# RWKV-7 recurrence: alpha and key times a stored by the inverse stage and loaded by the recurrence, y normalised on ScalarE

## The chip, the cores and the metric

The kernel runs on one core of one Trainium2 chip. The metric is the device time of one execution in microseconds (us), and of several executions the median. A core has TensorE (PE, with a separate stream of weight loads, PEld), VectorE (DVE), ScalarE (ACT), GpSimd (POOL) and SyncE (SP). In this kernel SP issues the DMA transfers between DRAM and the on-chip memory.

## The reference, cut to what matters

The reference is one inference step of a trunk with two layers. Layer 0 is a gated DeltaNet, layer 1 is RWKV-7 time mixing with D = 1024 and 16 heads of 64. The input is one prompt of 16 + 1024 tokens and 8 sample sequences of 8 tokens. The change touches layer 1 alone, and there the recurrence and the group norm behind it:

```python
kk = l2norm((k * k_k).reshape(B, T, H, N))
k = k * (1.0 + (a - 1.0) * k_a)
decay = jnp.exp(-jnp.exp(w))
b_h = kk * a_h

def step(S, inp):
    r_t, k_t, v_t, d_t, kk_t, b_t = inp
    S = (S * d_t[:, :, None, :]
         + jnp.einsum('bhvk,bhk->bhv', S, -kk_t)[..., None] * b_t[:, :, None, :]
         + v_t[..., None] * k_t[:, :, None, :])
    return S, jnp.einsum('bhvk,bhk->bhv', S, r_t)

S, y = lax.scan(step, S0, ...)
mean = jnp.mean(y, -1, keepdims=True)
var = jnp.mean(jnp.square(y - mean), -1, keepdims=True)
y = (y - mean) * lax.rsqrt(var + GN_EPS) * lnx_w + lnx_b
y = y + jnp.sum(r_h * k_h * r_k, -1, keepdims=True) * v_h
y = y.reshape(B, T, D) * jax.nn.silu(z)
return y @ w_o, S, xn[:, -1]
```

Every token's state update depends on the one before. The kernel does it in chunks of 64 tokens. Within a chunk, with D the running product of the decays, it uses four scaled rows: alpha = kk times D of the token before, r times D, k divided by D, and kk times a divided by D. Products of these give the triangular matrices of a chunk, and one of them has to be inverted.

## The kernel before, in words

All tokens stand in 1104 columns, cut into three segments of 384, 384 and 336. The 16 RWKV heads are taken in 8 pairs, one head in each half of the 128 partitions. A head pair in one segment is an item; there are 24 of them, numbered 8 times the segment plus the pair, and each has six chunks of 64.

Layer 0 takes the first 1380 us or so of the span. Layer 1 then has two stages.

In the first, up to about 1850 us, `layer1` makes the projections of the keys with decay and rate, then 24 calls of `project` for r, v and the gate's part z. They are numbered 0 to 23; each multiplies one 1024x128 block of weights with all columns and stores its result to DRAM (rd, vd, zd). `load_w` (L198) brings such a block in two halves of 256 KB (tile wraw, 2 buffers); ACT casts the high part (whi, L86), POOL makes the low part (wlo, L90), and PE uses both (3 buffers each). A half block takes part in 36 matmuls. Behind projections 0, 3, 6, 9 and 12 `rwkv_inverse` treats a batch of five items (the last one four). Per item it loads decay sums, a and k, makes kk (ACT), D and 1/D (`Dp`, `iD`, ACT), alpha (tile sal, DVE L1280, with small copies on POOL), kk times a (POOL L1305) and that over D (tile skk, DVE L1306), and multiplies them on PE: 12 small matmuls fL, with three more, frss, for the norms of kk. The result goes through DRAM (store L1319) into blocks of 32x32 of all items of the batch. DVE inverts these row by row (L448 and L450, a chain of 31 steps for all blocks at once), the results go through invA and DRAM to the tiles r_t and r_u (loads L472 and L471), and PE merges them to inverses of 64x64 (mU, mY), which are stored to ttd (L1332). In this stage a scheduler with a model of the times sets the order of every engine. SP has one queue, and carries out its issues in that order: the weights, the loads of the items, the stores.

The second stage, from about 1850 us to the end, is `wave`: the recurrence. It runs over steps tau from -3 to 54; item n has its chunk ci at step tau = 2n + ci, so three items are under way at a time, and a new one begins every second step. The order on PE is written out by hand, that on the other engines is the scheduler's. For each item:

- `rwkv_front` runs ahead, at tau 2n-4. It loads decay sums, k, a, r and v, makes kk, D and 1/D again, and from them the tile AR (alpha, POOL L1280 to L1283, and r times D, DVE L1358) and the tile BK (k over D, DVE L1365, and kk times a over D, POOL L1362 and L1366). AR has 5 buffers, BK has 2.
- At tau 2n-2 and 2n-1 the parts follow: the products BK by AR, masked into G (DVE L1395, L1397), the bonus (pr L1371, rbv L1380), values into UV, the inverse from ttd, and BK transposed into BT (L1407).
- `step_solve` to `step_state` do a chunk: PE products into rA, ACT makes X and UV and the scaled old state pre (all L62) and copies y (L1490; L1488 on DVE for the first chunk), DVE updates the state S (L1484, L1486).
- `rwkv_finish`, at the last chunk: mean and variance (DVE L1503 and L1504), the inverse root (`rsqrt`, tile grs, L103 to L106), and y minus mean times grs, chunk by chunk on POOL (L1509). Then PE transposes y (fyT), and DVE applies weight, bonus and gate (L1516, L1517).

`fill` puts matmuls of the gate and output projections (zz, zo, do) between these on PE, so that PE need not wait for the recurrence. The sums of the output projections go through DRAM (zst, L1591 to L1607), and the final norm is in `finish` (f2k L1638, dfin).

Of the kernel before, what the change touches and what calls it, by code (L numbers as in the profile page):

```python
# [10 lines left out]
AF = mybir.ActivationFunctionType  # L11
ALU = mybir.AluOpType
# [23 lines left out]
class Builder:  # L36
# [1211 lines left out]
    def rwkv_open(self):  # L1248
        self.rk2 = self.t(self.cp, [128, 144], "rk2")
        self.csd, self.ad, self.rd, self.vd, self.zd, self.kd = (self.dram([8, 128, 1152], n) for n in  # L1250
                                                                 ("csd", "ad", "rd", "vd", "zd", "kd"))
        self.ttd = self.dram([24, 128, 384], "ttd")

    def rwkv_load(self, n, pool, tag, names):
        nc, t = self.nc, self.t
# [9 lines left out]
    def rwkv_keys(self, p, ld, pool, tag):  # L1265

        nc, t = self.nc, self.t
        kk = t(pool, [128, 384], tag + "kk", 2 if tag == "s" else 1)
        self.act(kk, ld["k"], AF.Identity, scale=self.pcol["rwkv_k_k"][:, p:p + 1])
        Dp, iD = t(pool, [128, 385], tag + "Dp", 1), t(pool, [128, 384], tag + "iD", 1)  # L1270
        nc.gpsimd.memset(Dp[:, 0:1], 1.0)
        self.act(Dp[:, 1:385], ld["cs"], AF.Exp, scale=-self.DEC)
        self.act(iD, ld["cs"], AF.Exp, scale=self.DEC)
        return kk, Dp, iD

    def alpha(self, al, kk, Dp, s, eng):

# [10 lines left out]
    def rwkv_inverse(self, b, pool):  # L1288

        items = range(5 * b, min(5 * b + 5, 24))  # L1290
        nth = 6 * len(items)
        nc, t = self.nc, self.t
        ltd, ssd = self.dram([nth, 128, 64], f"rltd{b}"), self.dram([nth, 128], f"rssd{b}")
        for q, n in enumerate(items):
            s, p = divmod(n, 8)
            names = ("cs", "a", "k")
            ld = self.ahead or self.rwkv_load(n, pool, "s", names)
            kk, Dp, iD = self.rwkv_keys(p, ld, pool, "s")

            self.ahead = self.rwkv_load(n + 1, pool, "s", names) if n < 23 else None  # L1300
            sq = t(pool, [128, 384], "sgl", 2)
            self.act(sq, kk, AF.Square)
            al = t(pool, [128, 6, 64], "sal", 1)
            self.alpha(al, kk, Dp, s, nc.vector)
            nc.gpsimd.tensor_tensor(kk, kk, ld["a"], op=ALU.mult)  # L1305
            nc.vector.tensor_tensor(kk, kk, iD, op=ALU.mult)  # L1306
            gp = self.ps("f", 2, "L")
            ssp = self.ps("f", 2, "rss")
            for c in range(6):
                for h in (0, 1):  # L1310
                    a = 64 * h
# [13 lines left out]
        rk2 = self.rk2[:, 30 * b:30 * b + nth]  # L1325
        blk = self.block_scale(ssd, rk2, pool)
        TT = [t(pool, [128, 6, 64], "sTT", 3) for _ in items]
        T1n, L21 = t(pool, [128, 30, 32], "T1n", 1), t(pool, [128, 30, 32], "L21", 1)
        self.inverse_blocks(f"r{b}", ltd, blk, pool, TT, T1n[:, 0:nth], L21[:, 0:nth], nth)
        for q, n in enumerate(items):  # L1330
            self.inverse_merge(L21, TT[q], T1n, rk2[:, 6 * q:6 * q + 6], pool, 6 * q, 6)
            nc.sync.dma_start(self.ttd[n], TT[q].rearrange("p c k -> p (c k)"))  # L1332


    def rwkv_front(self, p, s):

        nc, t, ap, fp, col = self.nc, self.t, self.ap, self.fp, self.pcol
        P = Ctx()
        P.p, P.s, P.n = p, s, 8 * s + p
        NB = self.NB  # L1340
# [6 lines left out]
                q = slice(64 * h, 64 * h + 64)  # L1347
                nc.sync.dma_start(P.TT[q, h].rearrange("p c k -> p (c k)"), self.ttd[P.n][q])
        ld = self.rwkv_load(P.n, fp, "f", ("cs", "k", "a", "r", "v"))
        kk, Dp, iD = self.rwkv_keys(p, ld, fp, "f")  # L1350
        DC = P.DC = t(fp, [128, 14], "DC", NB + 2)
        nc.gpsimd.tensor_copy(DC[:, 0:6].unsqueeze(2), Dp[:, 1:385].rearrange("p (c k) -> p c k", k=64)[:, :, 63:64])
        if s == 0:
            nc.gpsimd.tensor_copy(DC[:, 6:14].unsqueeze(2), Dp[:, 1:65].rearrange("p (c k) -> p c k", k=8)[:, :, 7:8])
        AR = P.AR = t(fp, [128, 6, 2, 64], "AR", NB + 1)
        c6 = lambda x: x.rearrange("p (c k) -> p c k", k=64)
        self.alpha(AR[:, :, 0, :], kk, Dp, s, nc.gpsimd)
        nc.vector.tensor_tensor(AR[:, :, 1, :], c6(ld["r"]), c6(Dp[:, 1:385]), op=ALU.mult)  # L1358
        k2 = t(fp, [128, 384], "k2", 1)
        self.act(k2, ld["a"], AF.Identity, scale=pc("rwkv_k_a"), bias=self.omka[:, p:p + 1])  # L1360
        nc.vector.tensor_tensor(k2, k2, ld["k"], op=ALU.mult)
        nc.gpsimd.tensor_tensor(kk, kk, ld["a"], op=ALU.mult)  # L1362

        BK = t(fp, [128, 6, 2, 64], "BK", 2)
        nc.vector.tensor_tensor(BK[:, :, 0, :], c6(k2), c6(iD), op=ALU.mult)  # L1365
        nc.gpsimd.tensor_tensor(BK[:, :, 1, :], c6(kk), c6(iD), op=ALU.mult)  # L1366
        flat = lambda x: x.rearrange("p x k -> p (x k)")
        yield P

# [14 lines left out]
        def scores(c):  # L1384

            gp = [self.ps("f", 2, "G") for h in (0, 1)]
            for u in range(3):
                for h in (0, 1):
                    q = slice(64 * h, 64 * h + 64)
                    self.mm(gp[h][:, 128 * u:128 * u + 128], flat(BK[q, c + u]), flat(AR[q, c + u]))  # L1390
            for h in (0, 1):
                g3 = gp[h][:, 0:384].rearrange("p (q k) -> p q k", k=128)
                f = 0
                if s == 0 and c == 0:
                    nc.vector.tensor_tensor(G[:, 0, h, :], g3[:, 0, :], self.gms, op=ALU.mult)  # L1395
                    f = 1
                nc.vector.tensor_tensor(G[:, c + f:c + 3, h, :], g3[:, f:3], self.gm.unsqueeze(1).broadcast_to([128, 3 - f, 128]),  # L1397
                                        op=ALU.mult)
# [26 lines left out]
    def step_solve(self, P, ci):  # L1425

        nc, t, ap = self.nc, self.t, self.ap
        c = 6 * P.s + ci
        if ci == 0:
            P.y = t(ap, [128, 6, 64], "y", 4)  # L1430
        AR, S = P.AR, self.S[P.p]
        pA = P.pA = self.ps("r", 3, "A")
        X = P.X = t(ap, [128, 64], "X", 4)
        hs = [slice(0, 64), slice(64, 128)]
        if c > 1:
            for h in (0, 1):
                self.mmx(pA[hs[h], 0:64], AR[hs[h], ci, 0], S[hs[h]], True)
            for h in (0, 1):
                self.mmx(pA[hs[h], 256:320], AR[hs[h], ci, 1], S[hs[h]])

    def step_scores(self, P, ci):
        nc, t, ap = self.nc, self.t, self.ap
# [49 lines left out]
    def rwkv_finish(self, p, s, P):  # L1492

        nc, t, ap, col = self.nc, self.t, self.ap, self.pcol
        c0, n = SEGS[s]
# [4 lines left out]
        mv = t(ap, [128, 6, 2], "mv", 2)  # L1500
        y6 = y
# [3 lines left out]
        va, rs = t(ap, [128, 6], "va", 2), t(ap, [128, 6], "grs", 2)  # L1505
        nc.vector.tensor_scalar(va, mv[:, :, 1], GN_EPS, None, op0=ALU.add)
        self.rsqrt(rs, va, ap, "gn")
        for q in range(6):
            nc.gpsimd.tensor_scalar(y6[:, q], y6[:, q], mv[:, q, 0:1], rs[:, q:q + 1], op0=ALU.subtract, op1=ALU.mult)  # L1509
        yield  # L1510
        yp = self.ps("f", 2, "yT")
        for q in range(6):
# [16 lines left out]
    def rwkv_sample_read(self, P):  # L1529

        nc, t, ap = self.nc, self.t, self.ap
        p, AR = P.p, P.AR
# [12 lines left out]
        rp = self.ps("d", 2, "rsr")  # L1545
        for b in range(8):
            for h in (0, 1):
                a = 64 * h
                self.mm(rp[a:a + 64, 16 * b:16 * b + 16], P.Sb[a:a + 64, b, :], AR[a:a + 64, 0, :, 8 * b:8 * b + 8])
# [368 lines left out]
```

## Time and profile before

| What | Value |
|---|---|
| Runs | 2364.39, 2366.5 and 2373.59 us, median 2366.5 |
| Profiled execution | 2368.36 us, of which the span of the trace is 2366.6 |
| Mean granted TensorE clock | 0.969 |
| PE busy | 2187.2 us, 92% of the span |
| DVE, ACT, POOL busy | 68%, 54%, 46% |
| Bytes moved by the hardware DMA queue | 286.53 MB |

A group of instructions is told by line, engine, operation, the tile written and the tiles read, with its count, busy time, mean duration of one in ns and the idle time of its engine just before it. A wait row says which instruction waited, and for which engine, tile and line. A timeline row gives start, duration, engine, line, operation and tiles; in square brackets stands the wait just before it. The granted clock is the share of full speed that the throttle let TensorE have.

### The profile page before, as it was taken

Reading aid. Unit: us, or ns where it says so; the run is one execution under the profiler, and the core shown is the slowest. Engines: PE = TensorE matmul, PEld = TensorE weight load, DVE = VectorE, ACT = ScalarE, POOL = GpSimd, SP = SyncE. Lnnn points to the kernel's source line nnn. Section 1 sums busy time; section 2 is a strip of 40 time slices with the busy share of each in tenths; the row PEclk is TensorE's granted clock in tenths of the full one; section 3 lists DMA queues with packets and bytes.
Section 4 is the critical chain, followed back from the end, with each engine's and each line's share of the span. In section 5 each row is a group of like instructions: output and inputs, shape, how many; then the busy total and the mean of one; then the engine's idle time right before and its main releaser. Section 6 shows DMA issues by size and latency. Waiting matters only on the chain. (4 is left out here: it accounts for less than half of the span.)

```text
span 2366.6 us, 55058 instructions
## 1 busy us (share of the span) xinstructions
PE 2187.2 (92%) x19833; PEld 1991.7 (84%) x19833; DVE 1605.3 (68%) x4201; ACT 1283.9 (54%) x3665; POOL 1095.3 (46%) x1542
## 2 busy tenths in 40 slices
PE   6989999999999999999999999998899998999896
PEld 5878988888898989887989999897788877778785
DVE  6868668695857686783335833479786566778754
ACT  5455546464655555556333655646444455667663
POOL 3435334443434343444131532545344656777764
PEclk9999999999999999999999999999999989999998
DMA  3324333323233333336153154566754544565544
GB/s 113 106 67 112 83 85 83 108 68 103 87 90 94 88 110 89 85 94 192 50 151 94 44 165 163 169 162 176 203 140 132 176 112 139 159 186 177 176 145 128
DMA packets 471019, 290.06 MB, mean 123 GB/s; under 512 B 188601, under 2 KB 456122, under 8 KB 470746
## 3 DMA queue, kind: packets, MB, share of 16 engines
q1 hardware_dynamic: 470746, 286.53, 42.9%
q8 instruction: 157, 2.57, 0.5%
q14 instruction: 116, 0.95, 0.1%
HBM read 200.53 MB, written 85.89 MB: 121 GB/s over the span
## 5 line engine op out<-in xcount | busy, mean ns | idle before, releaser
L90 POOL TENSOR_TENSOR wlo<-wraw,whi 128x512 fp32r<-128x512 f32 (+2 forms) x252 | 328.0, 1304 | 348.0 <-ACT whi L86 334.1
L76 PE MATMUL d<-xc,whi 128*128 128x384 f32 (+2 forms) x910 | 258.1, 340 | 12.0 <-ACT whi L86 6.7
L86 ACT CAST whi<-wraw 128x512 fp32r<-128x512 f32 (+2 forms) x252 | 151.7, 603 | 139.5 <-PE dq L76 50.6
L415 DVE SCALAR_TENSOR_TENSOR cvy<-raw,cw,cvy 128x408 f32<-128x408 f32 (+2 forms) x288 | 179.5, 637 | 17.2 <-ACT cvy L62 15.4
L76 PEld LDWEIGHTS d<-xc,whi 128*128 128x128 f32 (+1 forms) x910 | 167.7, 191 | 16.7 <-ACT whi L86 7.3
L448 DVE TENSOR_TENSOR invtmp<-invA,invT 72x31 f32<-72x31 f32 (+31 forms) x403 | 166.0, 412 | 14.0 <-DMA invA<-ltd 4.4
L450 DVE TENSOR_TENSOR invT<-invT,invtmp 72x31 f32<-72x31 f32 (+31 forms) x403 | 166.4, 413 | 6.5
L76 PE MATMUL dz<-xc,whi 128*128 128x384 f32 (+1 forms) x480 | 149.9, 343 | 0.0
L76 PE MATMUL dv<-xc,whi 128*128 128x384 f32 (+1 forms) x480 | 146.8, 335 | 0.0
L76 PE MATMUL d<-xc,wlo 128*128 128x384 f32 (+2 forms) x428 | 142.8, 343 | 1.0 <-POOL wlo L90 0.9
L76 PE MATMUL d<-xa,whi 128*128 128x384 f32 (+3 forms) x450 | 139.2, 344 | 4.2 <-DVE xa L90 1.8
L864 POOL TENSOR_SCALAR Sb<-Sb,eglb 128x128 f32<-128x128 f32 x128 | 81.8, 656 | 85.4 <-DMA Sb<-in_state_gdn 29.3
L1509 POOL TENSOR_SCALAR y<-y,mv,grs 128x64 f32<-128x64 f32 x144 | 84.1, 601 | 37.4 <-DVE grs L106 35.8
L76 PE MATMUL dz<-xa,whi 128*128 128x384 f32 (+1 forms) x288 | 101.3, 352 | 0.0
L76 PE MATMUL dv<-xa,whi 128*128 128x384 f32 (+1 forms) x288 | 100.1, 347 | 0.1
L76 PEld LDWEIGHTS dz<-xc,whi 128*128 128x128 f32 x480 | 89.8, 193 | 0.8
L76 PEld LDWEIGHTS d<-xa,whi 128*128 128x128 f32 (+1 forms) x450 | 83.2, 190 | 8.2 <-DVE xa L90 2.4
L76 PEld LDWEIGHTS dv<-xc,whi 128*128 128x128 f32 x480 | 88.6, 188 | 0.5 <-issue 0.4
L76 PE MATMUL d<-xa,wlo 128*128 128x384 f32 (+3 forms) x252 | 86.4, 343 | 0.8 <-POOL wlo L90 0.8
L62 ACT ACTIVATE o<-rA,gcol 128x128 f32<-128x128 f32 x128 | 46.7, 372 | 73.0 <-DVE S L775 72.6
L76 PE MATMUL d<-xh,wlo 128*128 128x384 f32 (+1 forms) x256 | 83.5, 341 | 2.0 <-POOL wlo L90 1.9
L76 PEld LDWEIGHTS d<-xc,wlo 128*128 128x128 f32 (+1 forms) x428 | 80.8, 190 | 4.1 <-issue 1.8
(508 smaller groups left out, 7221.8 us busy)
## 6 DMA issues: line engine op xcount, KB each, us to landing
wraw<-in_gdn_w_in SPq DMA_DIRECT2D x96, 256.0 KB
wraw<-in_rwkv_w_rkvz SPq DMA_DIRECT2D x80, 256.0 KB
Sb<-in_state_gdn SPq DMA_DIRECT2D x64, 256.0 KB
wraw<-in_rwkv_w_o SPq DMA_DIRECT2D x40, 256.0 KB
E<-drow SPq DMA_DIRECT2D x24, 384.0 KB
attn<-drow SPq DMA_DIRECT2D x24, 384.0 KB
wraw<-in_gdn_w_out SPq DMA_DIRECT2D x36, 256.0 KB
out_s_gdn<-Sb SPq DMA_DIRECT2D x32, 256.0 KB
```

The costliest lines, as they stand in the source:

```text
L62: return self.nc.scalar.activation(out, in_, func, bias=bias, scale=scale, **kw)
L76: self.nc.tensor.matmul(out, lhsT, rhs, start=start, stop=stop)
L86: nc.scalar.copy(hi, x)
L90: e.tensor_tensor(lo, x, hi.bitcast(F32), op=ALU.subtract)
L415: nc.vector.scalar_tensor_tensor(y[:, 0:wd], raw[:, k:k + wd], cw[k], y[:, 0:wd], op0=ALU.mult, op1=ALU.add)
L448: nc.vector.tensor_tensor(tmp, A[:, j, j + 1:32].unsqueeze(2).broadcast_to([nb, n, m]), Tv[:, j, 0:m].unsqueeze(1).broadcast_to([nb, n, m] ...
L450: nc.vector.tensor_tensor(Tv[:, j + 1:32, 0:m], Tv[:, j + 1:32, 0:m], tmp, op=ALU.subtract)
L864: nc.gpsimd.tensor_scalar(Sb[:, u], Sb[:, u], self.eglb[:, hv, 4 * g + u:4 * g + u + 1], None, op0=ALU.mult)
L1509: nc.gpsimd.tensor_scalar(y6[:, q], y6[:, q], mv[:, q, 0:1], rs[:, q:q + 1], op0=ALU.subtract, op1=ALU.mult)
```

## The change

The inverse stage stores what it makes anyway: alpha (sal) to a new DRAM tensor ald, and kk times a over D (skk) to bkd, 192 KB each, for all 24 items; 48 stores on SP. `rwkv_front` no longer makes kk, alpha, kk times a and BK's second half, but loads alpha into AR and the other into BK, 48 loads on SP, the latter in runs of 256 bytes. It still makes D and 1/D, r times D and k over D. AR is laid out with alpha and r times D as two planes of six chunks (before, the two stood side by side in each chunk). The tile of kk has two buffers in the one place where it remains, as before. In `rwkv_finish` DVE makes nm = -mean times grs, one instruction per item on 128x6 elements, and the six normalisations per item, 144 in all, are activations on ScalarE with scale grs and bias nm.

By engine, in instructions of the built programs: DVE 4131 to 4155, ACT 3424 to 3544, POOL 1547 to 1299, SP 1922 to 2018; PE has 14353 in both.

```diff
-        self.ttd = self.dram([24, 128, 384], "ttd")
+        self.ttd, self.ald, self.bkd = (self.dram([24, 128, 384], n) for n in ("ttd", "ald", "bkd"))
...
     def rwkv_keys(self, p, ld, pool, tag):
-        kk = t(pool, [128, 384], tag + "kk", 2 if tag == "s" else 1)
+        kk = t(pool, [128, 384], tag + "kk", 2)
         self.act(kk, ld["k"], AF.Identity, scale=self.pcol["rwkv_k_k"][:, p:p + 1])
+        return kk, *self.rwkv_decays(ld, pool, tag)
+
+    def rwkv_decays(self, ld, pool, tag):
         Dp, iD = t(pool, [128, 385], tag + "Dp", 1), t(pool, [128, 384], tag + "iD", 1)
         nc.gpsimd.memset(Dp[:, 0:1], 1.0)
         self.act(Dp[:, 1:385], ld["cs"], AF.Exp, scale=-self.DEC)
         self.act(iD, ld["cs"], AF.Exp, scale=self.DEC)
-        return kk, Dp, iD
+        return Dp, iD
...
             self.alpha(al, kk, Dp, s, nc.vector)
             nc.gpsimd.tensor_tensor(kk, kk, ld["a"], op=ALU.mult)
             nc.vector.tensor_tensor(kk, kk, iD, op=ALU.mult)
+            nc.sync.dma_start(self.ald[n], al.rearrange("p c k -> p (c k)"))
+            nc.sync.dma_start(self.bkd[n], kk)
...
-        kk, Dp, iD = self.rwkv_keys(p, ld, fp, "f")
+        Dp, iD = self.rwkv_decays(ld, fp, "f")
...
-        AR = P.AR = t(fp, [128, 6, 2, 64], "AR", NB + 1)
+        AR = P.AR = t(fp, [128, 2, 6, 64], "AR", NB + 1)
+        BK = t(fp, [128, 6, 2, 64], "BK", 2)
+        nc.sync.dma_start(AR[:, 0].rearrange("p c k -> p (c k)"), self.ald[P.n])
+        nc.sync.dma_start(BK[:, :, 1, :], self.bkd[P.n].rearrange("p (c k) -> p c k", k=64))
-        self.alpha(AR[:, :, 0, :], kk, Dp, s, nc.gpsimd)
-        nc.vector.tensor_tensor(AR[:, :, 1, :], c6(ld["r"]), c6(Dp[:, 1:385]), op=ALU.mult)
+        nc.vector.tensor_tensor(AR[:, 1], c6(ld["r"]), c6(Dp[:, 1:385]), op=ALU.mult)
...
-        nc.gpsimd.tensor_tensor(kk, kk, ld["a"], op=ALU.mult)
-        BK = t(fp, [128, 6, 2, 64], "BK", 2)
         nc.vector.tensor_tensor(BK[:, :, 0, :], c6(k2), c6(iD), op=ALU.mult)
-        nc.gpsimd.tensor_tensor(BK[:, :, 1, :], c6(kk), c6(iD), op=ALU.mult)
...
+        nm = t(ap, [128, 6], "gnm", 2)
+        nc.vector.scalar_tensor_tensor(nm, mv[:, :, 0], -1.0, rs, op0=ALU.mult, op1=ALU.mult)
         for q in range(6):
-            nc.gpsimd.tensor_scalar(y6[:, q], y6[:, q], mv[:, q, 0:1], rs[:, q:q + 1], op0=ALU.subtract, op1=ALU.mult)
+            self.act(y6[:, q], y6[:, q], AF.Identity, scale=rs[:, q:q + 1], bias=nm[:, q:q + 1])
```

The reads of AR in `scores`, `step_old` and the sample read follow the new layout. Every file line behind the first edit moves by a few.

More of the change, by code (lines that the diff above doesn't have):

```diff
@@ L1267, in rwkv_keys @@
         nc, t = self.nc, self.t
-        kk = t(pool, [128, 384], tag + "kk", 2 if tag == "s" else 1)
+        kk = t(pool, [128, 384], tag + "kk", 2)
         self.act(kk, ld["k"], AF.Identity, scale=self.pcol["rwkv_k_k"][:, p:p + 1])
+        return kk, *self.rwkv_decays(ld, pool, tag)
+    def rwkv_decays(self, ld, pool, tag):
+        nc, t = self.nc, self.t
         Dp, iD = t(pool, [128, 385], tag + "Dp", 1), t(pool, [128, 384], tag + "iD", 1)
@@ L1389, in scores @@
                     q = slice(64 * h, 64 * h + 64)
-                    self.mm(gp[h][:, 128 * u:128 * u + 128], flat(BK[q, c + u]), flat(AR[q, c + u]))
+                    self.mm(gp[h][:, 128 * u:128 * u + 128], flat(BK[q, c + u]), AR[q, :, c + u])
             for h in (0, 1):
@@ L1436, in step_solve @@
             for h in (0, 1):
-                self.mmx(pA[hs[h], 0:64], AR[hs[h], ci, 0], S[hs[h]], True)
+                self.mmx(pA[hs[h], 0:64], AR[hs[h], 0, ci], S[hs[h]], True)
             for h in (0, 1):
-                self.mmx(pA[hs[h], 256:320], AR[hs[h], ci, 1], S[hs[h]])
+                self.mmx(pA[hs[h], 256:320], AR[hs[h], 1, ci], S[hs[h]])
     def step_scores(self, P, ci):
@@ L1548, in rwkv_sample_read @@
                 a = 64 * h
-                self.mm(rp[a:a + 64, 16 * b:16 * b + 16], P.Sb[a:a + 64, b, :], AR[a:a + 64, 0, :, 8 * b:8 * b + 8])
+                self.mm(rp[a:a + 64, 16 * b:16 * b + 16], P.Sb[a:a + 64, b, :], AR[a:a + 64, :, 0, 8 * b:8 * b + 8])
         q = t(ap, [128, 2, 8, 8], "rkst", 1)
```

## The prediction

> **What bounds the kernel now.** I read the busy shares first, then busy time by stretches of 100 us, then what TensorE (PE) waited for in layer 1, then the timeline at the two places that the change touches.
>
> ```profile
> PE 2187.2 (92%) x19833; PEld 1991.7 (84%) x19833; DVE 1605.3 (68%) x4201; ACT 1283.9 (54%) x3665; POOL 1095.3 (46%) x1542
> ```
>
> ```profile
> 1600.00:1700.00 100.00, 90.18 (x1045) 80.42 (x1044) 90.31 (x205) 59.59 (x135) 44.70 (x66) 0.95 0.67 179
> 1700.00:1800.00 100.00, 86.86 (x975) 77.89 (x976) 84.26 (x189) 50.57 (x107) 45.63 (x59) 0.95 0.58 148
> 2100.00:2200.00 100.00, 90.34 (x1315) 78.59 (x1315) 80.42 (x218) 66.67 (x214) 76.33 (x98) 0.97 0.61 183
> ```
>
> PE is the bound, at 92% of the span. Columns of the stretches: length, busy PE, PEld, DVE, ACT, POOL, granted clock, DMA share, GB/s. In both stages of the change (inverses about 1500 to 1760, recurrence about 1850 to 2366) PE has 10 to 13 us idle in 100. DVE is second in the inverse stage; in the recurrence DVE and POOL lie close together. Work taken off POOL therefore buys time only where PE waits for it or for what it holds up. What PE waits for, inverse stage first (total, times, longest):
>
> ```profile
> PE d L76 <- ACT whi L86: 6.7, 2, 6.1
> ```
>
> ```profile
> PE fBT L73 <- DVE G L1397: 11.8, 13, 1.2
> PE zz L76 <- DVE zst L1033: 5.3, 2, 2.7
> PE rA L80 <- ACT y L1490: 4.8, 15, 1.0
> PE zo L76 <- DVE zst L1605: 4.5, 3, 2.8
> PE dfin L73 <- DVE f2k L1638: 4.1, 1, 4.1
> PE rA L80 <- DVE y L1488: 2.1, 1, 2.1
> PE do L76 <- DVE f2k L1638: 2.0, 1, 2.0
> ```
>
> The first is a late projection weight; the rest is the recurrence, nearly all behind DVE, none behind POOL.
>
> **The inverse stage: 48 stores in front of the weights.** SP issues loads, stores and weight loads in one fixed order. The change adds two stores of 192 KB per head pair and segment (ald, bkd), and a store waits until DVE has made alpha and kk·a·iD, holding all behind it on SP. The scheduler also moves the weight loads back. Places on SP in the two built programs, half projections:
>
> ```
> weight load    before  after        weight load    before  after
> 12, 1st half   1144    1177         13, 2nd half   1226    1316
> 12, 2nd half   1158    1255         14, 1st half   1236    1318
> 13, 1st half   1224    1292         14, 2nd half   1253    1347
> ```
>
> In the new order, place 1254, just ahead of the second half of projection 12, is a load of r_u, which needs the finished 32x32 inverses of the third batch. Before, this half was far ahead of it:
>
> ```profile
> 1665.98 1.41 SPq L198 DMA_DIRECT2D wraw<-in_rwkv_w_rkvz  x1
> 1702.20 0.42 PE L76 MATMUL frss<-sgl,hmask 128*32 128x128 f32 x6 [0.36 <-DVE invtmp L448]
> 1703.28 0.43 SPq L198 DMA_DIRECT2D wraw<-in_rwkv_w_rkvz  x1
> 1705.69 0.59 SPq L471 DMA_DIRECT2D r_u<-invA  x1
> 1708.68 1.29 PE L76 MATMUL d<-xc,whi 128*128 128x384 f32 x3 [6.07 <-ACT whi L86]
> 1715.32 0.34 PE L76 MATMUL d<-xh,whi 128*128 128x384 f32 x1
> 1715.49 0.34 PE L76 MATMUL d<-xh,wlo 128*128 128x384 f32 x1
> 1717.85 0.92 PE L76 MATMUL fL<-sal,skk 64*64 64x64 f32 x24
> 1718.69 0.42 PE L76 MATMUL frss<-sgl,hmask 128*32 128x128 f32 x6
> 1725.89 0.54 PE L76 MATMUL mU<-sTT,invY 32*32 32x32 f32 x19
> 1726.33 0.48 PE L76 MATMUL mY<-T1n,L 32*32 32x32 f32 x19
> ```
>
> Prices from these rows. The issues at 1665.98 and 1703.28 are places 1158 and 1224: 37.30/66 = 0.565 us each. Issue to first matmul: 1708.68-1703.28 = 5.4. Matmuls follow each other by 1715.49-1715.32 = 0.17 (0.175 taken), so a half projection, 36 matmuls, is 6.3. A gram group (fL, frss) is 1719.11-1717.85 = 1.26; a merge (mU, mY) about 0.9. The waiting PE was done at 1702.62.
>
> Built order after, as arrival against need. *Stall 1*: PE finishes the first half of projection 12 as before, at 1702.62 less the second half (6.3), one gram group (1.25) and about 1 of short waits = 1694.0; two gram groups and a transpose (2.6) cover up to 1696.6. The weight issues right behind r_u, 1705.69+0.6 = 1706.3, and reaches PE at 1711.7: 15.1 lost. *Stall 2*: 1292-1255 = 37 places, 20.9 us, issue at 1727.2, at PE 1732.6; PE is done at 1711.7+6.3+0.4 = 1718.4, with 5.1 of cover (two grams, three merges): 9.1. *Stall 3*: 24 places, 13.6, at PE 1746.2; PE ready at 1732.6+6.3+2.5 = 1741.4: 4.8. *Stall 4*: 31 places beyond, 17.5, at PE 1763.7; PE ready, two halves and two merges on, at 1760.9: 2.8. Sum 31.8, less the old 6.1 that this replaces: **+25.7**. At 0.43 us a place (the shorter issue above) the stalls are 15.1, 4.1, 1.5 and 0: +14.6. At 0.70 (0.565 and a quarter, an estimate, for stores that wait for their data; the weight issues above spread from 0.43 to 1.41) they are 44.2: +38.1. An inversion chain that ends 5 us sooner or later moves each by 5; one cause would be sal, which has one buffer, so that DVE's next alpha waits until the ald store has landed. I take that wait at zero, since the scheduler lays one head's chain under the next; were SP 5 us late with such a store, DVE, busy 90 of 100 here, and the inverses behind it would be 5 late.
>
> A long stall also costs clock (same columns, 2 us each):
>
> ```profile
> 1706.00:1708.00 2.00, 0.00 (x0) 0.00 (x0) 0.56 (x1) 0.52 (x2) 0.78 (x1) 0.50 0.87 282
> ...
> 1710.00:1712.00 2.00, 2.00 (x31) 1.50 (x31) 0.44 (x1) 0.58 (x2) 2.00 (x2) 0.50 0.81 205
> 1712.00:1714.00 2.00, 2.00 (x13) 2.00 (x11) 1.86 (x8) 1.54 (x4) 0.75 (x5) 0.84 1.04 211
> ```
>
> After the 6.07 us wait PE ran at 0.50 from 1708.68 to about 1712.5, some 2 us lost. Of the new stalls two more are that long: +3 to 4. Against this go short waits for the merges, about 3 us, that lie hidden in the stalls. **Inverse stage: +26**, ends +11 and +43. In the Trainium skill, "TensorE: Matmul & The Clock Gate", Part 1: The HAM clock gate, an idle window of about 3.4 us halves the clock until about as long a busy one; the trace agrees, with 0.50 for 3.8 us after the stall, and by the page stalls 1 to 3 would pay, some 1 us more than I take.
>
> **The recurrence.** One head pair follows another, PE-bound. A period:
>
> ```profile
> 2106.15 0.55 PE L73 MATMUL fBT<-ident,BK 128*128 128x128 f32 x3 [1.03 <-DVE G L1397]
> 2110.98 0.73 ACT L62 ACTIVATE X<-rA,rk 128x64 f32<-128x64 f32 x3 [1.34 <-PE rA L80]
> 2111.40 0.17 DVE L106 SCALAR_TENSOR_TENSOR grs<-gn_t,grs 128x6 f32<-128x6 f32 x1
> 2112.45 0.74 ACT L62 ACTIVATE UV<-rA 64x128 f32<-64x128 f32 x3 [0.74 <-PE rA L80]
> 2114.41 0.34 PE L80 MATMUL rA<-UV,BT 128*64 128x64 f32 x4
> 2116.94 0.44 ACT L1490 COPY y<-rA 128x64 f32<-128x64 f32 x3
> 2117.20 0.92 PE L80 MATMUL rA<-rS,AR 64*64 64x64 f32 x24 [0.28 <-ACT y L1490]
> 2122.61 0.55 PE L73 MATMUL fBT<-ident,BK 128*128 128x128 f32 x3 [1.02 <-DVE G L1397]
> ```
>
> The spread of the DVE multiplications in this stage (minimum, median, maximum in ns), and groups of instructions (busy us, mean ns | idle before):
>
> ```profile
> L1358 DVE TENSOR_TENSOR AR<-fldr,fDp x24: 548/1597/3396, 1843.9 to 2255.0; 128x384 f32<-128x384 f32 x24
> L1365 DVE TENSOR_TENSOR BK<-k,fiD x24: 534/1318/3693, 1845.5 to 2258.2; 128x384 f32<-128x384 f32 x24
> ```
>
> ```profile
> L1509 POOL TENSOR_SCALAR y<-y,mv,grs 128x64 f32<-128x64 f32 x144 | 84.1, 601 | 37.4 <-DVE grs L106 35.8
> L62 ACT ACTIVATE fkk<-fldk,pcol 128x384 f32<-128x384 f32 x21 | 12.9, 612 | 0.8 <-DMA fldk<-kd 0.8
> ```
>
> ```profile
> L62 ACT ACTIVATE o<-rA,gcol 128x128 f32<-128x128 f32 x128 | 46.7, 372 | 73.0 <-DVE S L775 72.6
> ```
>
> The period is 2122.61-2106.15 = 16.46 us, 1.02 of it a wait for the masked scores G.
>
> *Removed from POOL*: alpha with its small copies, kk·a and BK1 per pair, and all six normalisations (84.1 us). No PE wait above names POOL; the gain goes by DVE. The same DVE multiplication takes 0.55 us at its quickest and 1.6 and 1.3 in the median (L1358, L1365): nearly 2 us a pair in these two alone. With POOL nearly empty, I take the G wait to go (-11.8), and about 5 of the other 21.0 - 4.8 = about 16 us behind DVE: **-17**. Ends: 0, if those durations have another cause, and -32.8 with every wait of that list but the weights'. The Trainium skill, "SBUF — State Buffer", on two separate sides, says a DVE operation with two SBUF inputs and a GpSimd operation that reads SBUF exclude each other for the whole instruction; the 548 and 1597 ns agree. By that rule alone all DVE-made waits could go, which is rival B.
>
> *nm on DVE*: 24 of the size of the grs row, 0.17 each, 4 us, beside PE. It delays the normalisation, 2111.40+0.17+0.17 = 2111.74.
>
> *Six normalisations on ACT*: no row shows one. Nearest are the X activation of the same size, 0.73/3 = 0.24 each, and the o one with twice the elements, 0.37: six are 1.45 to 2.2; I take 1.8, between. Against it fkk leaves ACT (0.61, once a pair, elsewhere in the period). In the built order these six stand between X and UV of the next even step. X ends at 2111.71, nm is there at 2111.74, so UV, which started at 2112.45, starts about 2113.6 (+1.2). The state matmul that needs UV ran at 2114.41, just covered; but the y copies behind slip from 2116.94 to about 2117.6, and PE's wait for y grows from 0.28 to about 0.94. For 16 of the pairs, 0.66 each: **+10.6** (ends 0.31 and 1.06 each: +5 and +17). Were nm late by 1 us or more, UV and all behind it would be late one for one: rival C.
>
> *New loads*: 48 of 192 KB on SP, ahead of their use by most of a period and bounded by that at zero; at 0.43 to 0.59 an issue SP gains some 1 us a period, and the DMA share is 0.61. If late, the first score matmul waits, not longer than the old POOL chain. *AR's layout*: same elements per matmul; zero.
>
> Sum: -17+11 = **-6**, ends -28 and +17; I keep -20 to +6 as likely.
>
> **Sum.** +26-6 = +20. The profiled execution took 2368.4 (span 2366.6), so 2388.4; it lies 1.9 above the median of 2366.5, so **2386.5**.
>
> **Rivals.** *A, the forecast*: weights late behind SP's queue, part won back; 2372 to 2402; 0.62. *B, other side*: the stalls for weights stay at 16 us together (+10), because r_u issues sooner than I work out, the y waits cost their low end (+5), and DVE's relief takes all of its 32.8: -18, 2349. For it: the widths of the DVE durations. Against: place 1254 is fixed, and no faster DVE takes it away. It decides from r_u issuing before about 1696; 0.13. *C, ScalarE becomes the bound*: nm arrives late and normalisations hold UV, 2.0 a pair on the path less 1.0 of the G wait, over 24 pairs +23, on top of the stalls (+26): +49, 2415. For it: ACT is at 67% in that stretch and order is fixed; against: X ends as nm arrives; 0.15. *D, nothing*: both hidden, 2366; 0.10.
>
> Chances: 0.5%, 12 us, is about what this kernel's measurement tells from no change. Faster, below 2354.7: three quarters of B, 0.10. Same: the rest of B, D, and 0.03 of A's lower tail, 0.16. Slower: 0.74. The range, 2364 to 2408, reaches past A's 2372 to the upper side of D and past A's 2402 into C's lower part, and leaves out B and most of C.
>
> **What would show it.** Right: a wait of PE for whi of over 8 us between about 1690 and 1735, with clock 0.5 after; the wait for G gone; L1358's median near 0.6; a longer wait for y. Wrong: r_u issuing much earlier, or waits for UV in every period.

## The result and the profile after

The changed kernel took 2386.59 us (median; 2384.75 to 2394.68) against 2366.92 for the kernel before beside it: a ratio of 1.0085, interval 1.0061 to 1.0108, or +20 us. The prediction was 2386.5; the five runs themselves lie 10 us apart.

The page's busy shares of the changed kernel, and then the same stretches of 100 us as before the change (length, busy PE, PEld, DVE, ACT, POOL, granted clock, DMA share, GB/s):

```profile
PE 2186.5 (92%) x19833; PEld 1994.4 (84%) x19833; DVE 1567.4 (66%) x4225; ACT 1316.4 (55%) x3785; POOL 920.7 (39%) x1294
```

```profile
1600.00:1700.00 100.00, 80.70 (x965) 72.52 (x966) 84.19 (x199) 52.84 (x117) 38.01 (x62) 0.91 0.66 182
1700.00:1800.00 100.00, 77.53 (x888) 69.34 (x884) 76.05 (x176) 40.74 (x88) 34.73 (x49) 0.84 0.61 159
2100.00:2200.00 100.00, 93.36 (x1388) 82.50 (x1384) 68.83 (x224) 77.16 (x253) 39.74 (x45) 0.98 0.72 210
```

PE has the same work, and the loss lies in the inverse stage. There PE was idle 9.8 and 13.1 us in the two stretches before and is idle 19.3 and 22.5 now, 18.8 more, and the clock fell from 0.95 to 0.91 and 0.84. In the recurrence PE is a little busier than before (90.34), POOL's load has halved, and ACT (77) is now the second engine.

What PE waits for in the changed kernel, first in the inverse stage, then in the recurrence (total, times, longest):

```profile
PE d L76 <- ACT whi L86: 12.5, 5, 6.3
PE fL L76 <- DVE skk L1311: 12.1, 8, 3.4
PE mU L76 <- ACT sTT L62: 6.9, 4, 4.7
PE fbpp L73 <- DVE invtmp L448: 6.6, 1, 6.6
...
PE rA L80 <- ACT y L1496: 11.9, 13, 1.9
PE rA L80 <- ACT X L62: 6.3, 9, 2.0
...
PE fG L76 <- DVE k L1524: 4.4, 8, 1.3
```

The late weights are there (12.5 against 6.7), but the inverse tiles (sTT) and a transpose (fbpp) are late as well, and the grams (fL) wait twice as long as before:

```profile
PE fL L76 <- DVE skk L1306: 6.3, 5, 2.4
```

In the recurrence the wait for G, 11.8 before, has left the list, and ScalarE's y and X have come in its place.

To compare stages between executions I use three points of PE: the start of the first gram, the start of the first state product of the recurrence, and the end of the span. Up to the first gram the programs are alike, yet it starts at 1485 to 1497 us in the traces below, so one span says less than the stages do. The rows of before, and then of after:

```profile
1495.83 0.33 PE L76 MATMUL fL<-sal,skk 64*64 64x64 f32 x2
...
1882.18 0.34 PE L80 MATMUL rA<-UV,BT 128*64 128x64 f32 x4
```

```profile
1485.33 0.33 PE L76 MATMUL fL<-sal,skk 64*64 64x64 f32 x2
...
1898.83 0.34 PE L80 MATMUL rA<-UV,BT 128*64 128x64 f32 x4
```

That is 386.3 us before and 413.5 after for the inverse stage, +27.2; and from there to the ends of the spans (2366.6 and 2383.0) 484.4 and 484.2, no difference. In the inverse stage so cut out PE was idle 31.0 us before and 51.3 after. Its matmuls, 3577 records in both, were busy for 355.4 and 362.2 us, at a mean granted clock of 0.96 and 0.91. Of the 27 us some 20 are thus longer waits, and 7 go with the lower clock.

### The profile page after: what moved, and what is told of

Its sections match the earlier page's. It is cut to its first block, busy times and chain, and to the rows that moved or that the text cites. A ratio compares the mean times of both kernels' runs of the same rounds, so it can differ in the third digit from the quotient of the medians.

```text
span 2383.0 us, 55113 instructions
## 1 busy us (share of the span) xinstructions
PE 2186.5 (92%) x19833; PEld 1994.4 (84%) x19833; DVE 1567.4 (66%) x4225; ACT 1316.4 (55%) x3785; POOL 920.7 (39%) x1294
## 5 line engine op out<-in xcount | busy, mean ns | idle before, releaser
L415 DVE SCALAR_TENSOR_TENSOR cvy<-raw,cw,cvy 128x408 f32<-128x408 f32 (+2 forms) x288 | 180.6, 640 | 17.3 <-ACT cvy L62 15.5
L76 PE MATMUL d<-xa,whi 128*128 128x384 f32 (+3 forms) x450 | 141.6, 348 | 12.4 <-ACT whi L86 9.4
L76 PE MATMUL d<-xl,whi 128*128 128x384 f32 (+1 forms) x256 | 84.3, 346 | 1.9 <-POOL xl L90 1.4
L62 ACT ACTIVATE attn<-attn,gcol 128x128 f32<-128x128 f32 x144 | 46.8, 391 | 69.2 <-POOL attn L575 65.1
```

Source lines behind the costliest of these rows:

```text
L62: return self.nc.scalar.activation(out, in_, func, bias=bias, scale=scale, **kw)
L76: self.nc.tensor.matmul(out, lhsT, rhs, start=start, stop=stop)
L415: nc.vector.scalar_tensor_tensor(y[:, 0:wd], raw[:, k:k + wd], cw[k], y[:, 0:wd], op0=ALU.mult, op1=ALU.add)
```

## The experiments

All runs in one table. A ratio of 0.001 is 2.4 us.

| Run | Ratio to before [95%] | Inverse stage, us | Recurrence, us |
|---|---|---|---|
| before | 1 | 386.3 | 484.4 |
| changed kernel | 1.0085 [1.0061, 1.0108] | 413.5 | 484.2 |
| ynorm_alone | 1.0075 [1.0051, 1.0100] | 387.0 | 498.4 |
| norm_after_uv | 1.0138 [1.0116, 1.0160] | 386.6 | 518.9 |
| norm_after_y | 1.0104 [1.0077, 1.0130] | 387.0 | 504.8 |
| norm_dve | 0.9964 [0.9945, 0.9983] | 390.3 | 479.7 |
| stores_alone | 1.0101 [1.0064, 1.0138] | 408.0 | 482.3 |
| stores_ready | 1.0103 [1.0072, 1.0135] | 407.8 | 480.2 |
| stores_half | 1.0039 [1.0019, 1.0059] | 403.9 | 480.2 |
| stores_act_queue | 1.0120 [1.0079, 1.0162] | 414.4 | 483.8 |
| stores_pool_queue | 1.0095 [1.0073, 1.0116] | 406.7 | 493.4 |
| weights_first | 1.0109 [1.0074, 1.0143] | 407.8 | 489.2 |
| loads_no_norm | 1.0007 [0.9990, 1.0024] | 407.5 | 466.9 |
| one_store | 0.9963 [0.9942, 0.9984] | 401.4 | 465.2 |

Inverse stages that no edit touches (before, ynorm_alone, norm_after_uv, norm_after_y, norm_dve) lie between 386.3 and 390.3. Each column is one execution: the two together differ from the medians by up to 8 us either way (the changed kernel +27 by the columns, +20 by the medians; ynorm_alone +15 and +18; stores_alone +20 and +24), so a column tells where the time goes, and a ratio how much.

### The change taken apart: the normalisation, the stores, the loads

`ynorm_alone`, the normalisation on ScalarE and nothing else:

```diff
         for q in range(6):
-            nc.gpsimd.tensor_scalar(y6[:, q], y6[:, q], mv[:, q, 0:1], rs[:, q:q + 1], op0=ALU.subtract, op1=ALU.mult)
+            self.act(y6[:, q], y6[:, q], AF.Identity, scale=rs[:, q:q + 1], bias=nm[:, q:q + 1])
```

> The kernel before, with only the normalisation of y moved from GpSimd to ScalarE (and nm on VectorE). The inverse stage keeps its order to the instruction, so only the recurrence can move. My steps: six normalisations ahead of UV make the waits for y longer, +10.6; half of GpSimd's relief comes from this move, so half of -17: -8. Sum +2, 2369 (2362 to 2380), with the wait of TensorE for y well above the 4.8 us of before. If ScalarE became the bound (rival C): +23, 2390, with waits for UV in every period. If the relief outweighs it: 2357.

`stores_alone`, the 48 stores added to the kernel before and nothing that loads them:

```diff
             nc.vector.tensor_tensor(kk, kk, iD, op=ALU.mult)
+            nc.sync.dma_start(self.ald[n], al.rearrange("p c k -> p (c k)"))
+            nc.sync.dma_start(self.bkd[n], kk)
```

> The kernel before, with only the 48 stores of alpha and key times a added in the inverse stage; nothing loads them, and the recurrence is as before. Theory of the queue: the whole cost of the change is here, +20 to +26 in the inverse stage and nothing in the recurrence: 2387 to 2393, at or above the changed kernel. Rival (the stores are hidden, and the changed kernel pays in the recurrence for its loads and for ScalarE): 2367.

`loads_no_norm`, the changed kernel with the normalisation back on GpSimd:

```diff
         for q in range(6):
-            self.act(y6[:, q], y6[:, q], AF.Identity, scale=rs[:, q:q + 1], bias=nm[:, q:q + 1])
+            nc.gpsimd.tensor_scalar(y6[:, q], y6[:, q], mv[:, q, 0:1], rs[:, q:q + 1], op0=ALU.subtract, op1=ALU.mult)
```

> The changed kernel with the normalisation of y back on GpSimd: stores, loads and the dropped products remain. The inverse stage is that of stores_alone (+25 by the trace). In the recurrence, if the relief of GpSimd by the dropped products gains by itself: the wait for G (11.8 before) falls below 4 and the recurrence is 8 to 17 us shorter than before, 2369 to 2378. Rival (only the normalisation's leaving frees VectorE, the loads gain nothing): recurrence as before, 2385.

Measured: 2380.12, 2384.83 and 2368.33 us. The normalisation by itself costs 0.75%, 18 us, against my +2; the stores cost 1.0%, 24 us, as expected; stores with loads cost nothing, so the loads and the products that they replace give about 22 back. By the stages: the stores +21.7, the loads 466.9-484.4 = -17.5, the normalisation +14.0 alone and 484.2-466.9 = +17.3 on top of the loads. The change as a whole is stores +22 to 24, loads -18 to -22, normalisation +17 to 18.

What PE waits for in the recurrence of ynorm_alone, and then of loads_no_norm:

```profile
PE rA L80 <- ACT y L1490: 19.3, 16, 2.1
PE rA L80 <- ACT X L62: 7.5, 10, 2.0
PE fG L76 <- DVE k L1518: 6.1, 5, 2.3
...
PE fBT L73 <- DVE G L1397: 2.7, 6, 0.5
```

```profile
PE rA L80 <- DVE y L1494: 6.8, 3, 2.6
...
PE rA L80 <- ACT y L1496: 1.8, 4, 0.5
PE rA L80 <- ACT X L62: 1.8, 6, 0.4
```

The normalisation's leaving GpSimd does free VectorE: the wait for G falls from 11.8 to 2.7. But y rises by 14.5, X (1.8 before) by 5.7 and k (1.8 before) by 4.3. The loads remove the wait for G too; in the list of loads_no_norm only the wait for VectorE's y is much longer than before (6.8 against 2.1, three waits). So in the changed kernel the normalisation has no wait for G left to remove, and only its cost remains. VectorE's multiplications show which GpSimd work they collide with (mean ns of one after the bar and comma; first before, then loads_no_norm, then the changed kernel):

```profile
L1358 DVE TENSOR_TENSOR AR<-fldr,fDp 128x384 f32<-128x384 f32 x21 | 30.6, 1459 | 1.0 <-ACT fDp L62 0.5
L1365 DVE TENSOR_TENSOR BK<-k,fiD 128x384 f32<-128x384 f32 x21 | 26.8, 1278 | 0.1
```

```profile
L1367 DVE TENSOR_TENSOR AR<-fldr,fDp 128x384 f32<-128x384 f32 x22 | 37.7, 1714 | 0.6 <-ACT fDp L62 0.3 <-DMA fldr<-rd 0.3
L1372 DVE TENSOR_TENSOR BK<-k,fiD 128x384 f32<-128x384 f32 x22 | 14.7, 666 | 0.1
```

```profile
L1367 DVE TENSOR_TENSOR AR<-fldr,fDp 128x384 f32<-128x384 f32 x22 | 22.9, 1040 | 6.1 <-ACT fDp L62 6.1
L1372 DVE TENSOR_TENSOR BK<-k,fiD 128x384 f32<-128x384 f32 x22 | 14.9, 675 | 0.1
```

BK, 1278 ns on average before, runs at 666 and 675 as soon as GpSimd's products are gone; r times D, 1459 before, is at 1714 as long as the normalisation is on GpSimd, and falls to 1040 when it leaves. The rule that the prediction cites, of the Trainium skill, "SBUF — State Buffer", on two separate sides, agrees with these six rows.

### Where the normalisation costs: its place on ScalarE

ScalarE over one even step of the changed kernel, the chunk's instructions alone:

```profile
2108.53 0.72 ACT L62 ACTIVATE X<-rA,rk 128x64 f32<-128x64 f32 x3 [1.34 <-PE rA L80]
2109.35 2.10 ACT L62 ACTIVATE y<-y,gnm,grs 128x64 f32<-128x64 f32 x6
2111.47 0.60 ACT L62 ACTIVATE UV<-rA 64x128 f32<-64x128 f32 x3
...
2115.31 0.44 ACT L1496 COPY y<-rA 128x64 f32<-128x64 f32 x3
```

The six stand between X and UV, without a gap: UV starts 2.22 us after X's end, where it was 0.74 before. PE's next old-state product then waits for the y copies:

```profile
2115.57 0.92 PE L80 MATMUL rA<-rS,AR 64*64 64x64 f32 x24 [1.14 <-ACT y L1496]
```

That wait was 0.28 before; I had worked out 0.94. Two runs moved the six elsewhere. In `norm_after_uv` they are emitted one even step later, behind X, UV and pre:

```diff
+        yield
         for q in range(6):
             self.act(y6[:, q], y6[:, q], AF.Identity, scale=rs[:, q:q + 1], bias=nm[:, q:q + 1])
...
                 each(self.step_state)
+                if tau % 2 == 0 and 0 <= (tau - 6) // 2 < 24:
+                    next(P[(tau - 6) // 2].done)
```

> The kernel before with the normalisation of y on ScalarE, but emitted one even step later, so that in ScalarE's order the six activations stand behind X, UV and the old state pre of that step, and no longer ahead of X or UV. Inverse stage as before. If the place in ScalarE's order is what cost the 18 us of ynorm_alone: the waits for y (19.3) and X (7.5) fall to under 10 and 3, while the wait for G (2.7) stays small, so 2361 before becomes 2350 to 2361. Rival (ScalarE is simply too full, or nm and the inverse root come too late on VectorE): 2370 to 2380, little better than ynorm_alone.

Measured: 2399.46, the worst of all. In most steps the scheduler had put them ahead of four activations of the next item's front and of the y copies, and the copies are what the next step needs:

```profile
PE rA L80 <- ACT y L1490: 42.4, 20, 3.0
```

`norm_after_y` is the same with the six queued behind those copies:

```diff
-            nc.scalar.copy(P.y[:, ci], pA[:, 256:320])
+            self.ycopy = nc.scalar.copy(P.y[:, ci], pA[:, 256:320]).ins
...
                 if tau % 2 == 0 and 0 <= (tau - 6) // 2 < 24:
-                    next(P[(tau - 6) // 2].done)
+                    with self.tc.issue_after(self.ycopy) if items else ExitStack():
+                        next(P[(tau - 6) // 2].done)
```

> The kernel before with the normalisation of y on ScalarE, queued there right behind the copies of y of the next even step, so that between X and those copies nothing is added. norm_after_uv put it just ahead of the copies and TensorE's waits for y rose to 42.4. If ScalarE's stretch from X to the copy of y lies on the recurrence's path and the rest of its period does not: waits for y and X at about 5 and 2 as before, the wait for G small as in ynorm_alone, 2352 to 2362. Rival (ScalarE has no 1.8 us free anywhere in the step, so X of the odd step is late in its place): 2372 to 2400 with waits for X.

Measured: 2384.57. The waits for y and X did fall to 3.9 and 3.0, but not the time; the next thing on ScalarE is late in their place, the copies of the values into UV ahead of the scores (wait rows of norm_after_y):

```profile
PE fG L76 <- ACT UV L1414: 24.0, 20, 1.9
...
PE rA L80 <- ACT y L1490: 3.9, 12, 0.4
PE rA L80 <- ACT X L62: 3.0, 6, 1.6
```

So it is not one unlucky place: in three places tried, the six delayed whatever stood behind them. Nor is it that nm comes late from VectorE: ScalarE stood idle 18.6 us for nm in ynorm_alone, but 3.0 and 2.2 in these two runs, which cost no less. ScalarE is busy three quarters of the time, but much of its free time lies in gaps before X and UV in which it waits for PE. In the kernel before these are 48.4 us in 43 waits and 52.6 in 52, about 1 us each, while the six take 2.10. `norm_dve` puts the same six on VectorE:

```diff
-            nc.gpsimd.tensor_scalar(y6[:, q], y6[:, q], mv[:, q, 0:1], rs[:, q:q + 1], op0=ALU.subtract, op1=ALU.mult)
+            nc.vector.tensor_scalar(y6[:, q], y6[:, q], mv[:, q, 0:1], rs[:, q:q + 1], op0=ALU.subtract, op1=ALU.mult)
```

> The kernel before with the normalisation of y on VectorE (six operations of the same form per item), nothing else. GpSimd is relieved of the same 84 us as in ynorm_alone, ScalarE is untouched. If GpSimd's normalisation is what holds VectorE: the wait for G falls as in ynorm_alone (2.7), the waits for y stay at 5, VectorE carries 144 more operations of some 0.15 us: 2350 to 2361. Rival (VectorE is the second bound, so the work added there delays G and X): 2365 to 2375.

Measured: 2358.65 us against 2366.65, ratio 0.9964, faster than both kernels. The wait for G falls to 4.7 (I expected 2.7), and that for y rises to 9.0 (I expected 5). Each operation takes 342 ns, more than the 150 that I expected, and 39 us in all:

```profile
L1509 DVE TENSOR_SCALAR y<-y,mv,grs 128x64 f32<-128x64 f32 x144 | 38.9, 342 | 0.7
```

### Why the stores cost: tests of the queue

The prediction's place is in the trace. These are the changed kernel's SP issues and PE's waits around it:

```profile
1696.98 0.35 SPq L491 DMA_DIRECT2D invR<-rssd  x1
...
1700.85 1.33 SPq L471 DMA_DIRECT2D r_u<-invA  x1
1702.22 0.40 SPq L198 DMA_DIRECT2D wraw<-in_rwkv_w_rkvz  x1
...
1724.62 0.78 SPq L198 DMA_DIRECT2D wraw<-in_rwkv_w_rkvz  x1
```

```profile
1690.57 1.01 PE L76 MATMUL fL<-sal,skk 64*64 64x64 f32 x24 [2.56 <-DVE skk L1311]
1698.73 0.28 PE L73 MATMUL fbpp<-ident,invR 30*128 30x30 f32 x1 [6.57 <-DVE invtmp L448]
1707.37 1.29 PE L76 MATMUL d<-xa,whi 128*128 128x384 f32 x3 [6.31 <-ACT whi L86]
```

The weights go out right behind r_u, and PE waits 6.31 us for them. Just before, it waits 6.57 for fbpp. The row names VectorE, but fbpp reads invR, whose load SP issued at 1696.98, 1.75 us earlier, so I read this wait as one for that load. Next to it the clock (columns as above, 4 us each):

```profile
1702.00:1706.00 4.00, 0.00 (x0) 0.00 (x0) 1.94 (x5) 0.00 (x0) 1.11 (x2) 0.50 1.07 245
1706.00:1710.00 4.00, 2.43 (x8) 1.90 (x9) 3.69 (x10) 1.55 (x3) 1.38 (x1) 0.50 0.95 244
1710.00:1714.00 4.00, 4.00 (x30) 3.75 (x30) 3.55 (x9) 1.62 (x3) 1.37 (x3) 0.78 0.61 142
```

Three runs tried to give the time back by removing what seemed the cause. `weights_first`, on the changed kernel:

```diff
-        w = self.load_w(self.i["rwkv_w_rkvz"][0, m][:, 128 * k:128 * k + 128])
+        with self.tc.high_priority() if m == 2 and k in (4, 5, 6, 7) else ExitStack():
+            w = self.load_w(self.i["rwkv_w_rkvz"][0, m][:, 128 * k:128 * k + 128])
```

> The changed kernel with the weight loads of projections 12 to 15 (v, blocks 4 to 7) given high priority in the scheduler, so that the second half of projection 12 and both halves of 13 and 14's first half stand ahead of the third batch's r_u load on SyncE. All stores and loads stay. Theory of late weights: 12 to 20 us come back, 2367 to 2375, and the waits for whi around 1700 go. Rival (SyncE's issue rate itself is the limit, so that the inverse tiles come late in place of the weights): less than 6 us come back, 2381 to 2387, with waits for sTT, invR or skk in place of whi.

`stores_act_queue` and `stores_pool_queue`, each on the changed kernel (the second with `nc.gpsimd`):

```diff
-            nc.sync.dma_start(self.ald[n], al.rearrange("p c k -> p (c k)"))
-            nc.sync.dma_start(self.bkd[n], kk)
+            nc.scalar.dma_start(self.ald[n], al.rearrange("p c k -> p (c k)"))
+            nc.scalar.dma_start(self.bkd[n], kk)
```

> The changed kernel with its 48 stores issued by ScalarE's queue in place of SyncE's. Theory of the queue: the same bytes go out, but nothing on SyncE is pushed back by them; the inverse stage returns to within 8 us of before, and the recurrence keeps its gain of about 4: 2363 to 2374. Rival (the bytes written, or the waits of DVE for the store of sal, cost the time): the time stays at 2383 to 2390.

> The changed kernel with its 48 stores issued by GpSimd's queue. In this built order the weight loads of projections 12 to 15 and the r_u load stand within some 20 places of where they stand in the kernel before, unlike with ScalarE's queue, where r_u overtook both halves of projection 13. Theory of late weights: the inverse stage is within 10 us of before, total 2362 to 2374. Rival (the stores' bytes or sal's single buffer): 2380 or more, with the inverse chain of VectorE late.

All three missed: 2388.02, 2391.0 and 2387.5 us, as their rivals had it or 1 us above. What each bought, it gave back. With the weights first, PE's wait for them fell from 12.5 to 4.1, but SP issued r_u and invR of the next batch later, invR at 1724.00:

```profile
1710.06 0.33 SPq L471 DMA_DIRECT2D r_u<-invA  x1
1716.44 0.50 SPq L198 DMA_DIRECT2D wraw<-in_rwkv_w_rkvz  x1
...
1724.00 0.45 SPq L491 DMA_DIRECT2D invR<-rssd  x1
```

Batch 4's chain on VectorE started 234 us after the first gram and batch 5's ended at 335, where the changed kernel has 220 and 316. The inverse stage was 5.7 us shorter than the changed kernel's and the recurrence 5.0 longer, with PE's wait for k at 10.6 in place of 4.4. With ScalarE's queue, PE's longest wait was 9.3 us for T1n, which comes from r_t (12.4 in five waits). With GpSimd's, VectorE waited 23.5 us for GpSimd's product skk, where it waited 14.0 in the changed kernel and 11.7 before, and batch 4's chain took 62 us in place of 39 (35 before). VectorE's longest wait in the inverse stage of stores_pool_queue, and the same one in the changed kernel:

```profile
DVE skk L1311 <- POOL skk L1310: 23.5, 7, 4.8
```

```profile
DVE skk L1311 <- POOL skk L1310: 14.0, 10, 1.8
```

Late weights are thus one form that the cost takes, not its cause. The same holds for another late load: VectorE's chain waited 17.1 us for the small tile bblk in the changed kernel and 6.7 before, but only 9.7 in weights_first and 7.5 in stores_pool_queue, and the time stayed. Two more runs asked what about a store costs. `stores_ready` stores two tiles that have just been loaded, so that no store waits for a product and sal is not held; it waits for the load to land instead:

```diff
+            nc.sync.dma_start(self.ald[n], ld["k"])
+            nc.sync.dma_start(self.bkd[n], ld["a"])
             kk, Dp, iD = self.rwkv_keys(p, ld, pool, "s")
```

> The kernel before with 48 stores of the same size on SyncE in the inverse stage, but of the loaded key and rate tiles in place of alpha and key times a, so that no store waits for a product of VectorE and the single buffer sal is not held. Not the data that the change stores; nothing loads them. If issue slots and bytes on SyncE are the cost: 2385 to 2392, as stores_alone. If the waits for the products, or sal held until its store has landed, are the cost: 2367 to 2375.

`stores_half` is stores_alone without the second store:

```diff
             nc.sync.dma_start(self.ald[n], al.rearrange("p c k -> p (c k)"))
-            nc.sync.dma_start(self.bkd[n], kk)
```

> The kernel before with the 24 stores of alpha alone. If the cost goes with the number of stores: half of stores_alone's 24, 2375 to 2382. If it is a step (the built order tips, and the r_u load overtakes the weights): either 2387 as with 48, or 2367; here the second half of projection 12 stands ahead of r_u again and the next half right behind it, so a step would give about 2367 to 2372.

Measured: 2386.29 and 2371.28. The cost needs neither the waits for the products nor sal's single buffer: without both it is 22 us, as with them. But SP still stood at the stores. Its longest such waits, in stores_ready (slda and sldk are the loaded a and k) and then in stores_alone:

```profile
SPq L1299 <- DMA slda<-ad: 8.2, 8, 2.3
SPq L1298 <- DMA sldk<-kd: 7.9, 11, 1.8
```

```profile
SPq L1308 <- DVE invtmp L448: 8.8, 7, 3.2
SPq L1308 <- DVE invT L450: 6.4, 5, 2.9
```

With the shorter rows of the same lists that is 16.6 us in stores_ready, 22.6 in stores_alone and 9.4 in stores_half. That SP stands at a store and holds all behind it is therefore not excluded. Half the stores cost 0.39% (0.19 to 0.59), 9 us (4 to 14), where 48 cost 22 to 24; by the stage column it is 17.6 of 21.7. That half of the stores costs nothing, or all of it, is excluded by the ratio, though 2371.28 by itself lies in the range that I had given for a step: the kernel before took 2364.1 beside it. Whether the cost is in proportion is not settled.

Bytes and issues were told apart by `one_store`: loads_no_norm with alpha and key times a in one tile, and 24 stores of 384 KB in place of 48 of 192.

```diff
-            al = t(pool, [128, 6, 64], "sal", 1)
+            ab = t(pool, [128, 2, 384], "sal", 1)
+            al, bk = ab[:, 0].rearrange("p (c k) -> p c k", k=64), ab[:, 1]
...
-            nc.vector.tensor_tensor(kk, kk, iD, op=ALU.mult)
-            nc.sync.dma_start(self.ald[n], al.rearrange("p c k -> p (c k)"))
-            nc.sync.dma_start(self.bkd[n], kk)
+            nc.vector.tensor_tensor(bk, kk, iD, op=ALU.mult)
+            nc.sync.dma_start(self.abd[n], ab.rearrange("p x k -> p (x k)"))
```

> loads_no_norm with one store of 384 KB per item in place of two of 192 KB: alpha and key times a lie in one tile (one buffer), and go out in 24 stores. The recurrence loads them as in the changed kernel, y is normalised on GpSimd. Same bytes as the changed kernel, half its issues. If the cost of the inverse stage goes with issues on SyncE: as stores_half, +7 to +12, and with the recurrence's -22 the time is 2350 to 2358 against 2364 to 2367 before. Rival (the bytes, or the waits for the later of the two products, count): +22 in the inverse stage, 2364 to 2370, no better than before.

Measured: 2358.06 against 2365.76, ratio 0.9963 (0.9942 to 0.9984), faster than both kernels and 10 us better than loads_no_norm by the two ratios, with the same bytes. Its inverse stage is 401.4, beside 403.9 with 24 small stores and 407 to 414 with 48 on SP. So with the same bytes fewer stores cost less, and the bytes do not show. That the number of issues alone did it is not shown: SP also stood at the stores for 13.3 us in place of the 21.2 of loads_no_norm, and the scheduler built another order.

What stays open is how a store comes to cost some 0.45 us of the whole (22 us for 48), a little more than its 0.35 us on SP. Every edit that adds stores also makes the scheduler build the stage in another order. Taking the stores off SP brought nothing, but put them into the order of another engine. No run added stores with the order held fixed. Whether the slots on SP, its standing at the stores or the new orders cost the time was not separated.

## Why the prediction was right, and where its terms were not

- *Inverse stage +26 (ends +11 and +43)*: measured +27.2 by the columns, 22 to 24 by the medians of the runs with the stores alone. The size was right, the path only in part. The weight did go out right behind r_u, at 1702.22, and the next one 22.4 us later, where I had 20.9; r_u itself came at 1700.85, not 1705.7. But PE's wait for that weight was 6.3 us, not 15.1, and less than the 8 that I had named as a sign. The 6.57 us just before it are for another tile. All waits for whi together rose by 5.8 us (6.7 to 12.5), where my four stalls came to 25.7. As much came from the grams (+5.8), 6.9 from sTT and 6.6 from fbpp, none of which I had priced, and the lower clock cost 7, where I had 3 to 4. That these come to my sum is luck. The cause as put, weights late behind SP's queue, is one of the forms that the cost takes in this build: with the weights first the time stayed.
- *Recurrence -6*: measured -0.2 by the column, and -4 by the medians (+20 less 24 for the stores). Its two terms nearly cancelled, at -17.5 and +17.3 by the columns, where I had -17 and +10.6.
- *Relief of VectorE -17, G wait gone*: the wait went, and the relief was -17.5, but from the dropped products and the loads alone. I had shared one relief between these products and the normalisation; either of them is enough to end most of the wait for G (2.7 left in ynorm_alone), and what the second one adds is small. VectorE's r times D has a median of 903 ns in the changed kernel, not the 0.6 us that I had named as a sign. My sum of the list was also off: its waits other than G come to 22.8 us, not 21.0, with 18.0 behind VectorE, and the far end to -34.6, not -32.8. The relief was about half of either.
- *Normalisations on ScalarE +10.6*: this is the step that failed in size. Measured +14.0 alone, even with its relief for G, and +17.3 on top of the loads. The six took 2.10 us, inside my 1.45 to 2.2. Against loads_no_norm PE's wait for ScalarE's y rose by 10.1 us (1.8 to 11.9), about as I had it, while that for VectorE's y fell from 6.8 to 0.5. But I had not counted the waits for X, which rose by 4.5, and for k, by 2.6:

```profile
L62 ACT ACTIVATE y<-y,gnm,grs 128x64 f32<-128x64 f32 x144 | 50.5, 428 | 19.1 <-DVE gnm L1515 18.5
```

  The last entry says that ScalarE stood idle 18.5 us for nm before them, which I had taken as arriving in time (2111.74 against X's end at 2111.71). It was 14 waits, of up to 2.7 us.
- *nm on VectorE, new loads, AR's layout at zero*: no wait of PE names nm, AR or BK. nm was late for ScalarE all the same, as said.
- *Rivals.* B (the relief of VectorE outweighs the queue) fell: the relief was half of its 32.8. Of C (ScalarE becomes the bound) half came: nm was late and the normalisations cost +17, near its +23. But PE's waits for UV were 0.4 us in all, not one in every period, and the cost stood beside the relief. D fell.

The direction was earned: the stores' cost and the relief had about the right size. That the median came within 0.1 us of the forecast is luck, for the runs are 10 us apart, and the parts were less good than the sum. In the inverse stage the waits that I had priced were under a quarter of my number and others made it up, the normalisation was some 7 us too small, and the relief had the wrong owner.

## What to carry to other kernels

When one relief has two possible sources, price each as if the other had already happened; here either was enough, and beside the loads the one that added work to ScalarE was pure loss. An engine that is a quarter idle has room for an operation only if one of its gaps is long enough and nothing on the critical chain stands behind it in its queue: look at the timeline of one period, not at the share. Where a scheduler builds the order, price added stores together with the new order that they bring, try merging them before moving them to another queue, and test the late wait by moving it: if the time stays, the wait was where the cost showed and not what it came from.

## What the runs showed of the hardware that was not expected

An activation of 128x64 from SBUF to SBUF with a scale and a bias per partition took 428 ns on average, and six in a row 2.10 us. That of X, the same size from PSUM with a scale alone, took 310 ns, and three in a row 0.72 us. Which of the differences makes it was not tried. The normalisation took 601 ns on GpSimd (L1509 before) and 342 on VectorE, so moving it to ScalarE did not make it much quicker. With the stores on GpSimd's queue VectorE's waits for GpSimd's product skk were 23.5 us, against 14.0 in the changed kernel; whether the issuing or the new order made them longer was not tried.
